# Sending token numbers instead of rows to the experts, moving the closing gate steps, and splitting HGRN's heads earlier

## The chip, the cores and the metric

The kernel runs on one core of a Trainium2 chip. The metric is the device time of one execution in microseconds (us); lower is better. The engines that appear below are PE (TensorE, the matrix multiplies), DVE (VectorE), ACT (ScalarE), POOL (GpSimd, which here mostly issues DMAs) and SP (SyncE, which issues DMAs). All five run their own instruction streams and wait for one another by semaphores.

## The reference, cut to what matters

A decoder trunk of two layers on 512 tokens of width 1024, in float32. Layer 0 is an mLSTM mixer and a dense SwiGLU; layer 1, where the change lies, is an HGRN2 mixer and a top-2-of-8 mixture of experts:

```python
# layer 1
o = hgrn2_chunkwise(q, k, log_f, v)                 # 8 heads of 128
o = head_rmsnorm(o, norm_w) * silu(g)
x = x + gate1 * (o @ w_out)                         # "h_out" below
t = rmsnorm(x, norm2_w) * (1 + scale2) + shift2
logits = t @ router_w                               # 512 x 8
top_logits, top_idx = top_k(logits, 2)
top_w = softmax(top_logits)
gates = sum_k top_w * one_hot(top_idx, 8)
y = sum_e gates[:, e] * ((silu(t @ wg[e]) * (t @ wu[e])) @ wd[e])
x = x + gate2 * y                                   # then the final norm
```

## The kernel before

**Precision and tiles.** Every float32 matmul is made of two halves: a tile is split into a high part (made by ACT: whi of a weight, hhi of a head) and a low part (made by DVE: wlo, hlo), and PE multiplies high x high, low x high and high x low. The residual stream x lies in DRAM and in SBUF as 8 tiles of 128 features x 512 tokens. Weights come from DRAM in tiles of two slots (1024 KB), are split slot by slot by ACT and DVE, and run ahead of PE by a fixed number of slots; SP issues these loads (L189, raw<-in_w or raw<-in_moe), in the order in which buffers come free. All engine instructions carry the line of a helper, L337; DMAs have lines of their own.

**HGRN.** `hgrn()` computes projections tile by tile (`proj`), and between them, a few instructions at a time, the recurrence of each head (`core`); `weave` sets that order by a cost estimate when the program is written out. The finished head `hh[h]` (normed, turned by tph, multiplied with g) is wanted by `h_out`, which takes the heads in order k = 0..7: first the product of each head with four of eight output tiles (12 matmuls of 128x512 per head), later with the other four. `heads()` hands them over: per head one ACT step (hhi), one DVE step (hlo), and one DMA on POOL that reloads the residual tile of that number (L1291, xr<-X).

**Route.** After h_out the residual is turned to token-major tiles xt (128 tokens x 512 features, 4 x 2 of them) and normed to zt by eight ACT steps (`pre_route`). `route` finds for each token its two experts and its rank within each; an expert has room for 152 rows (CAP), so there are 8 x 152 = 1216 slots (NSLOT), and each token has a row beyond them where a choice without a slot is dumped. `spread()` makes the row numbers `put` on DVE; then 16 indirect DMAs on POOL (4 token tiles x 2 halves x 2 choices) write 128 rows of 2 KB each of zt into XG, in DRAM (L1465), with a tiny memset (spacer, L1464) in front of each. XG was filled with zeros earlier, beside the projections (L1113, 20 DMAs). `rest()` makes what is wanted late: the gates of rows without a slot, their count (cps on PE, n_over), the gate matrix GM in DRAM (a DMA on POOL, L1497), and lists of rows for the final adding.

**Experts.** `experts` runs expert 0 to 7. Expert 0 gets its rows without DRAM, by a product of xt with one-hot matrices. A step (e, i) of the first part multiplies with the gate and up weights of the i-th tile of hidden features (gu, 16 pairs of matmuls for each of the two), i = 0..10; the second part multiplies down (yd). For expert e+1, `fetch` loads its 152 rows at (e, 4) from XG, as four direct DMAs of 76 x 512 (L1623, xr<-XG); the turns xT at (e, 7), (e, 8) and (e, 9) transpose them on PE, features 0 to 383, 384 to 767 and the others. The results go to Y in DRAM and at the end are gathered per token by 16 indirect DMAs of 128 rows (L1757, yg<-Y,relse).

Of the kernel before, what the change touches and what calls it, by code (L numbers as in the profile page):

```python
# [10 lines left out]
F32 = mybir.dt.float32  # L11
F32R = mybir.dt.float32r
BF16 = mybir.dt.bfloat16
I32 = mybir.dt.int32
U32 = mybir.dt.uint32
AF = mybir.ActivationFunctionType
OP = mybir.AluOpType
# [4 lines left out]
P = 128  # L22
D = 1024
T = 512
KT = D // P
NC = T // P
H = 8
# [4 lines left out]
NE = 8  # L32
# [48 lines left out]
PLAN, AT = _plan()  # L81
# [12 lines left out]

CAP = 152
NSLOT = NE * CAP
NROW = NSLOT + 2 * T
NY = NSLOT - CAP


# [307 lines left out]
class Kernel:  # L408
# [637 lines left out]
    def hgrn(self):  # L1046
        nc, tc = self.nc, self.tc
        V, S = nc.vector, nc.scalar
        ident = self.C("ident")
        with ExitStack() as ctx:  # L1050
# [9 lines left out]
            e = one.tile([P, 3, 8], F32, name="lbs")  # L1060
# [42 lines left out]
            def proj():  # L1103
                accs = self.group_first("h_first", 4, self.norm(1, 0))
                self.dump("hn1", [x for h in self.hn for x in h])
                for k in range(KT):
                    nc.gpsimd.dma_start(self.X[k], self.x[k])
                z = self.nrm.tile([P, T], F32, name="zero", tag="tmp")
                nc.gpsimd.memset(z, 0.0)
                for j in range(2):  # L1110
                    for i in range(0, NSLOT, P):
                        n = min(P, NSLOT - i)
                        nc.gpsimd.dma_start(self.XG[j][i:i + n], z[:n])  # L1113
                evac(0, (accs[:2], accs[2:]))
                self.router()
                yield
                for what in H_ORDER:
                    w, n = what[0], int(what[1])
                    ps = []
                    for i in range(4):  # L1120
                        acc = self.ps(f"h{what}{i}")
                        if w == "h":
                            yield from self.tile_ws(AT[what] + 8 * i, self.hn, acc)
                            ps.append(acc)
                            if i == 3:
                                while not done >= {n - 3, n - 4}:
                                    yield "wait"
                                evac(n, (ps[:2], ps[2:]))
                            continue
                        t = new(f"{what}{i}", "vg", 12)  # L1130
                        if w == "v":
                            yield from self.tile_tok(AT["h_" + what], i, acc)
                            S.activation(t, acc, AF.Copy)
                            v[n, i] = t
                        else:
                            yield from self.tile_ws(AT["h_" + what] + 8 * i, self.hn, acc)
                            S.activation(t, acc, AF.Copy)
                            g[n + i] = t
                            if i >= 2:
                                gated(range(n + (i - 2) * 3, n + i + 1))  # L1140
# [138 lines left out]
                else:  # L1279
                    S.activation(t, tp, AF.Copy, scale=self.V("hnw", h))  # L1280

            def heads():
                for h in range(H):
                    while h not in hh or h not in on:
                        yield None
                    hi = self.act.tile([P, T], F32R, name=f"hhi{h}", tag="act")
                    lo = self.act.tile([P, T], F32R, name=f"hlo{h}", tag="act")
                    S.activation(hi, hh[h], AF.Copy)
                    V.tensor_sub(lo, hh[h], hi.bitcast(F32))
                    self.x[h] = self.xp.tile([P, T], F32, name=f"xr{h}", tag="x")  # L1290
                    nc.gpsimd.dma_start(self.x[h], self.X[h])  # L1291
                    yield hi, lo

            out = self.out_proj("h_out", heads(), 1, lambda: next(self.side, None))

# [22 lines left out]
    def pre_route(self, pool, lps, xt):  # L1318

        nc = self.nc  # L1320
        ident = self.C("ident")
        tp = {}

        lgt = self.ps("lgt")

        rw4 = self.nrm.tile([P, T], F32, name="rw4", tag="rs", bufs=1)[:, :(KT - 1) * 32].rearrange("p (k c) -> p k c", c=32)
        nc.gpsimd.memset(rw4, 0.0)
        nc.gpsimd.tensor_copy(rw4[:, :, 0:NE], self.rwa[:, 0:KT - 1])
        fold = pool.tile([P, NE], F32, name="fold")
        nc.vector.tensor_reduce(fold, ident.rearrange("p (g j) -> p j g", g=4)[:, 0:NE], axis=AX.X, op=OP.add)  # L1330

        def logits(*ks):

            mm = nc.tensor.matmul
            if ks[0] < KT - 1:
                for k in ks:
                    mm(lgt[32 * (k % 4):32 * (k % 4) + 32], rw4[:, k], self.x[k], start=k < 4, stop=k + 4 >= KT - 1)
                return
            k = ks[0]
            for i in range(NC):  # L1340
                ts = slice(i * P, (i + 1) * P)
                mm(lps[:, i], self.lgs[:, ts], fold, start=i == 0, stop=False)
            for i in range(NC):
                ts = slice(i * P, (i + 1) * P)
                mm(lps[:, i], self.x[k][:, ts], self.rwa[:, k], start=False, stop=i == NC - 1)
            next(scale, None)

        def turn(k, i):
            if (i, k // 4) not in tp:
                tp[i, k // 4] = self.ps(f"xt{i}{k // 4}")  # L1350
            nc.tensor.transpose(tp[i, k // 4][:, (k % 4) * P:(k % 4 + 1) * P], self.x[k][:, i * P:(i + 1) * P], ident)

        def evac(i, j):
            xt[i][j] = self.act.tile([P, 512], F32, name=f"xt{i}{j}", tag="act")
            if i % 2 or j:
                nc.scalar.activation(xt[i][j], tp.pop((i, j)), AF.Copy)
            else:
                nc.vector.tensor_copy(xt[i][j], tp.pop((i, j)))

        for i in range(NC):  # L1360
            for k in range(4):
                turn(k, i)
            if i == NC - 1:
                logits(*range(4))
            yield
            evac(i, 0)
            yield
        scale = self.token_scale()
        for k in range(4, KT):
            if k == KT - 2:  # L1370
                logits(*range(4, KT - 1))
            elif k == KT - 1:
                logits(k)
            for i in range(NC):
                turn(k, i)
            if k == KT - 2:
                self.lgs = pool.tile([P, T], F32, name="lgs")
                nc.vector.tensor_copy(self.lgs, lgt)
                next(scale)
            if k < KT - 1:  # L1380
                yield
                yield
                yield
        zt = [[None, None] for _ in range(NC)]
        for i in range(NC):
            evac(i, 1)
        for i in range(NC):
            for j in range(2):
                zt[i][j] = self.act.tile([P, 512], F32, name=f"zt{i}{j}", tag="act")
                nc.scalar.activation(zt[i][j], xt[i][j], AF.Copy, scale=self.rs[:, i:i + 1])  # L1390
        self.zt = zt

    def route(self, pool, lps, xt):
# [48 lines left out]
        def spread():  # L1442
# [14 lines left out]
            V.tensor_tensor(d2, dump, ok, op=OP.mult)  # L1457
            V.tensor_sub(d2, dump, d2)
            V.tensor_add(put, sl, d2)
            last, spacer = [], t("spacer", shape=[1, 1])  # L1460
            for i in range(NC):
                for j in range(2):
                    for c in range(2):
                        nc.gpsimd.memset(spacer, 0.0)  # L1464
                        st = nc.gpsimd.indirect_dma_start(  # L1465
                            out=self.XG[j], out_offset=bass.IndirectOffsetOnAxis(ap=put[:, c, i:i + 1], axis=0),
                            in_=self.zt[i][j], in_offset=None)
                        for x in last:
                            tc.declare_no_dep(st.ins, x.ins, reason="other rows")
                        last.append(st)  # L1470
            gate = t("gate", shape=[P, 2, NC])
            ex, den = t("ex", shape=[P, NC]), t("den", shape=[P, NC])
            V.tensor_sub(ex, m2, m1)
# [135 lines left out]
    def experts(self, xp, hp, wk, xt, pick, rest):  # L1609
# [6 lines left out]
        def fetch(e):  # L1616

            rows[e] = [[self.xp.tile([P, T], F32, name=f"xr{q}{j}{e}", tag="x")[:HC] for j in range(2)]
                       for q in range(2)]
            for q in range(2):  # L1620
                r0 = e * CAP + q * HC
                for j in range(2):
                    nc.gpsimd.dma_start(rows[e][q][j], self.XG[j][r0:r0 + HC])  # L1623

        def place(e):
            xs[e] = xp.tile([P, KT, 2, CAP], F32R, name=f"x{e}", tag="x")
# [137 lines left out]
        for kind, e, i in moe_steps():  # L1764
            if kind == "g":
# [4 lines left out]
                        self.mm2(gu[u], W.get(b), xs[e][:, k], k == 0, k == KT - 1)  # L1770
                        b += 1
                act(e, i, gu)
                if (e, i) == (0, 1):
                    g, r, n_over = rest()
                if e + 1 < NE:
                    if i == 4:
# [84 lines left out]

    def run(self, stop=None):
        tc, nc = self.tc, self.nc
        self.XG = [self.dram.tile([NROW, 512], F32, name=f"XG{j}") for j in range(2)]
        self.Y = [self.dram.tile([NY, 512], F32, name=f"Y{j}") for j in range(2)]
        self.YL = self.dram.tile([CAP, 512], F32, name="YL")
        self.X = self.dram.tile([KT, P, T], F32, name="X")
# [76 lines left out]
```

## Time and profile before

| | us |
|---|---|
| median of 3 runs | 1553.86 |
| lowest and highest | 1550.51, 1555.45 |
| the profiled execution's own time | 1556.14 |
| its span in the trace | 1554.4 |
| PE busy | 1488.2 (96%) |
| DVE, ACT, POOL busy | 1087.0, 845.6, 133.5 |
| mean granted PE clock, share of full speed | 0.985 |

The span is what the trace shows, from the first instruction to the last; the profiled execution's own time is a little longer and is one run among others. Times in rows are microseconds from the start of the span. The HGRN mixer ends at about 900, the experts run from about 975 to 1530. DVE, ACT and POOL have idle time nearly everywhere, PE hardly any.

### The profile page before, as it was taken

Reading aid. Unit: us, or ns where it says so; the run is one execution under the profiler, and the core shown is the slowest. Engines: PE = TensorE matmul, PEld = TensorE weight load, DVE = VectorE, ACT = ScalarE, POOL = GpSimd, SP = SyncE. Lnnn points to the kernel's source line nnn. Section 1 sums busy time; section 2 is a strip of 40 time slices with the busy share of each in tenths; the row PEclk is TensorE's granted clock in tenths of the full one; section 3 lists DMA queues with packets and bytes.
Section 4 is the critical chain, followed back from the end, with each engine's and each line's share of the span. In section 5 each row is a group of like instructions: output and inputs, shape, how many; then the busy total and the mean of one; then the engine's idle time right before and its main releaser. Section 6 shows DMA issues by size and latency. Waiting matters only on the chain.

```text
span 1554.4 us, 23601 instructions
## 1 busy us (share of the span) xinstructions
PE 1488.2 (96%) x8955; PEld 1308.3 (84%) x8955; DVE 1087.0 (70%) x1992; ACT 845.6 (54%) x1561; POOL 133.5 (9%) x217
## 2 busy tenths in 40 slices
PE   4989999999999999999999999999999999999995
PEld 3867777888888888788888877899999999999984
DVE  6876774655455645695977755787887878788786
ACT  5466333432222322365656554687786868777663
POOL 0041000000000000310000020501000010100141
PEclk9999999999999999999999999999999999999997
DMA  9472551445445553542102152778787787878782
GB/s 373 168 207 80 202 176 64 167 176 216 161 164 205 180 197 109 201 146 101 55 28 82 55 207 94 251 246 294 267 277 275 275 279 252 294 266 269 278 305 92
DMA packets 80903, 300.47 MB, mean 193 GB/s; under 512 B 8085, under 2 KB 8133, under 8 KB 79761
## 3 DMA queue, kind: packets, MB, share of 16 engines
q1 hardware_dynamic: 68608, 263.21, 48.0%
q0 software_dynamic: 12176, 35.70, 6.9%
q8 instruction: 72, 1.18, 0.3%
q14 instruction: 47, 0.38, 0.1%
HBM read 280.78 MB, written 18.09 MB: 192 GB/s over the span
## 4 chain that ended last, share of the span: by engine, by line
PE 86%; DVE 6%; ACT 3%; DMA 3%; issue 1%; DVEq 0%; SPq 0%; ACTq 0%
PE gu L337 22%; PE yd L337 11%; PE fd L337 8%; PE fgp L337 7%; PE fup L337 7%; PE hh L337 4%; PE al L337 3%; PE hv L337 3%; PE h_out L337 3%; PE m_g L337 3%; PE m_out L337 2%; PE hg L337 2%; PE o L337 1%; DMA ar<-in_ada 1%; PE f_in L337 1%
## 5 line engine op out<-in xcount | busy, mean ns | idle before, releaser
L337 DVE TENSOR_TENSOR wlo<-raw,whi 128x1024 fp32r<-128x1024 f32 x403 | 489.5, 1222 | 104.0 <-ACT whi L337 99.4
L337 ACT ACTIVATE whi<-raw 128x1024 fp32r<-128x1024 f32 x403 | 421.9, 1054 | 171.2 <-DMA raw<-in_w 36.4
L337 PE MATMUL gu<-x,whi 128*128 128x304 f32 x1408 | 362.0, 346 | 2.8 <-issue 1.0
L337 PE MATMUL gu<-x,wlo 128*128 128x152 f32 x1408 | 330.6, 235 | 1.5 <-issue 1.4
L337 PEld LDWEIGHTS gu<-x,wlo 128*128 128x128 f32 x1408 | 271.4, 193 | 2.5 <-issue 2.3
L337 PEld LDWEIGHTS gu<-x,whi 128*128 128x128 f32 x1408 | 267.1, 190 | 3.4 <-issue 1.6
L337 PE MATMUL yd<-hb,whi 128*128 128x304 f32 x704 | 181.5, 347 | 1.9 <-DVE hb L337 1.9
L337 PE MATMUL yd<-hb,wlo 128*128 128x152 f32 x704 | 164.1, 233 | 0.0
L337 PEld LDWEIGHTS yd<-hb,wlo 128*128 128x128 f32 x704 | 134.7, 191 | 0.0
L337 PEld LDWEIGHTS yd<-hb,whi 128*128 128x128 f32 x704 | 132.4, 188 | 2.3 <-DVE hb L337 2.3
L337 DVE SCALAR_TENSOR_TENSOR ar<-ar,cond 128x1024 f32<-128x1024 f32 x80 | 97.3, 1219 | 3.0 <-DMA ar<-in_ada 2.9
L337 ACT ACTIVATE fhi<-fg 128x512 fp32r<-128x512 f32 x22 | 13.9, 633 | 114.3 <-DVE fg L337 114.3
L337 DVE TENSOR_TENSOR fg<-fg,fup 128x512 f32<-128x512 f32 x20 | 13.8, 688 | 82.7 <-PE fup L337 82.7
L337 ACT ACTIVATE t<-gu 128x152 f32<-128x152 f32 x176 | 48.3, 289 | 42.2 <-PE gu L337 35.8
L337 PE MATMUL fd<-fhi,whi 128*128 128x512 f32 x176 | 69.6, 396 | 0.0
L337 PE MATMUL fd<-flo,whi 128*128 128x512 f32 x176 | 69.6, 396 | 0.0
L337 PE MATMUL fd<-fhi,wlo 128*128 128x512 f32 x176 | 69.6, 396 | 0.0
L337 PE MATMUL fgp<-lo,whi 128*128 128x512 f32 x160 | 62.3, 389 | 0.0
L337 PE MATMUL fgp<-hi,whi 128*128 128x512 f32 x160 | 62.2, 389 | 0.0
L337 PE MATMUL fgp<-hi,wlo 128*128 128x512 f32 x160 | 62.2, 389 | 0.0
L337 PE MATMUL fup<-hi,whi 128*128 128x512 f32 x160 | 62.2, 389 | 0.0
L337 PE MATMUL fup<-lo,whi 128*128 128x512 f32 x160 | 62.2, 389 | 0.0
(413 smaller groups left out, 2978.0 us busy)
## 6 DMA issues: line engine op xcount, KB each, us to landing
raw<-in_moe SPq DMA_DIRECT2D x125, 1024.0 KB, 5.2
raw<-in_w SPq DMA_DIRECT2D x69, 1024.0 KB, 6.0
ar<-in_ada SPq DMA_DIRECT2D x80, 512.0 KB, 4.3
ad<-in_ada SPq DMA_DIRECT2D x8, 1024.0 KB, 15.3
XG<-zero POOLq DMA_DIRECT2D x18, 256.0 KB
xr<-XG POOLq DMA_DIRECT2D x28, 152.0 KB
raw<-in_moe SPq DMA_DIRECT2D x8, 512.0 KB, 3.6
Y<-yt POOLq DMA_DIRECT2D x14, 256.0 KB
```

The lines of the kernel that those rows point to most:

```text
L337: r = f(*args, **kw)
```

## The change

Five things change. (1) XG is gone. SP writes zt to ZT in DRAM by token (2 x 512 x 512), each 128 x 512 tile right after the ACT step that makes it. (2) A list L of 2304 int32 takes XG's place: it is zeroed by one small DMA; DVE makes the token numbers `tok`; eight indirect DMAs scatter 128 of these numbers each to the rows `put`; and one DMA on POOL loads the first 1216 back as `who` (76 x 16). (3) `fetch` gathers an expert's rows from ZT by `who`, four indirect DMAs of 76 rows. (4) `rest()` is called after step (1, 6) in place of (0, 1). (5) The split of a head moves to `halves`, called within the last g tile for heads 0 and 1, and then three heads ahead of the one that is handed over.

```diff
@@ proj
-                for j in range(2):
-                    for i in range(0, NSLOT, P):
-                        n = min(P, NSLOT - i)
-                        nc.gpsimd.dma_start(self.XG[j][i:i + n], z[:n])
+                nc.gpsimd.dma_start(self.L.rearrange("(p k) o -> p (k o)", p=P), z[:, :NROW // P].bitcast(I32))
...
-                            yield from self.tile_ws(AT["h_" + what] + 8 * i, self.hn, acc)
+                            for k, r in enumerate(self.tile_ws(AT["h_" + what] + 8 * i, self.hn, acc)):
+                                yield r
+                                if n and i == 3 and k > 1:
+                                    halves(k - 1)
@@ heads
-            def heads():
-                for h in range(H):
-                    while h not in hh or h not in on:
-                        yield None
+            parts = []
+            def halves(n):
+                for h in range(len(parts), min(n, H)):
+                    if h not in hh or h not in on:
+                        return
                     hi = self.act.tile([P, T], F32R, name=f"hhi{h}", tag="act")
                     lo = self.act.tile([P, T], F32R, name=f"hlo{h}", tag="act")
                     S.activation(hi, hh[h], AF.Copy)
                     V.tensor_sub(lo, hh[h], hi.bitcast(F32))
                     self.x[h] = self.xp.tile([P, T], F32, name=f"xr{h}", tag="x")
                     nc.gpsimd.dma_start(self.x[h], self.X[h])
-                    yield hi, lo
+                    parts.append((hi, lo))
+            def heads():
+                for h in range(H):
+                    while h not in hh or h not in on:
+                        yield None
+                    halves(h + 3)
+                    yield parts[h]
@@ pre_route
                 nc.scalar.activation(zt[i][j], xt[i][j], AF.Copy, scale=self.rs[:, i:i + 1])
+                nc.sync.dma_start(self.ZT[j][i * P:(i + 1) * P], zt[i][j])
@@ spread
+            tok = self.nrm.tile([P, NC], I32, name="tok", tag="ms", bufs=1)
+            V.tensor_scalar(tok, dump[:, 0], -float(NSLOT), None, op0=OP.add)
             for i in range(NC):
-                for j in range(2):
-                    for c in range(2):
...
-                            out=self.XG[j], out_offset=bass.IndirectOffsetOnAxis(ap=put[:, c, i:i + 1], axis=0),
-                            in_=self.zt[i][j], in_offset=None)
+                for c in range(2):
...
+                        out=self.L, out_offset=bass.IndirectOffsetOnAxis(ap=put[:, c, i:i + 1], axis=0),
+                        in_=tok[:, i:i + 1], in_offset=None)
...
+            self.who = t("who", I32, [CAP // 2, 2 * NE])
+            nc.gpsimd.dma_start(self.who, self.L[0:NSLOT].rearrange("(s p) o -> p (s o)", p=CAP // 2))
@@ fetch
-                    nc.gpsimd.dma_start(rows[e][q][j], self.XG[j][r0:r0 + HC])
+                    nc.gpsimd.indirect_dma_start(
+                        out=rows[e][q][j], out_offset=None, in_=self.ZT[j],
+                        in_offset=bass.IndirectOffsetOnAxis(ap=self.who[:, 2 * e + q:2 * e + q + 1], axis=0))
@@ the loop of experts
-                if (e, i) == (0, 1):
+                if (e, i) == (1, 6):
                     g, r, n_over = rest()
```

ACT's queue from the last g tile of HGRN on, before (g<-hg takes the projection out of PSUM, g<-g is its silu; the hhi are heads 0, 1 and 2 in turn):

```order
L337 ACTIVATE g_6875<-hg_6874 128x512
L337 ACTIVATE g_6875<-g_6875 128x512
L337 ACTIVATE hhi_6925<-hh_5253 128x512
L337 ACTIVATE whi_6934<-raw_6779 128x1024
L337 ACTIVATE qi,ssqh<-o_6837 128x128 x4
L337 ACTIVATE qi<-o_6837,rshy 128x128 x4
L337 ACTIVATE hhi_6968<-hh_5308 128x512
L337 ACTIVATE hhi_6991<-hh_5908 128x512
```

There the hhi of head 0 waits behind both steps on g. ACT's queue of the change at the same place:

```order
L337 ACTIVATE hhi_6893<-hh_5235 128x512
L337 ACTIVATE hhi_6907<-hh_5290 128x512
L337 ACTIVATE g_6857<-hg_6856 128x512
L337 ACTIVATE g_6857<-g_6857 128x512
L337 ACTIVATE hhi_6919<-hh_5890 128x512
L337 ACTIVATE whi_6928<-raw_6761 128x1024
L337 ACTIVATE qi,ssqh<-o_6819 128x128 x4
L337 ACTIVATE hhi_6949<-hh_6019 128x512
L337 ACTIVATE qi<-o_6819,rshy 128x128 x4
```

The hhi of heads 0 and 1 now stand ahead of the last g<-hg, and that of head 2 stands right behind g<-g; a split of a weight, the square sums of the last head (qi,ssqh) and its scaling (qi<-o,rshy) come after these.

PE's queue where the last head is turned (tph), before, at the end of h_out's first two heads:

```order
L337 MATMUL h_out_6924<-hhi_6968,whi_6703 128x512
L337 MATMUL h_out_6924<-hlo_6969,whi_6703 128x512
L337 MATMUL h_out_6924<-hhi_6968,wlo_6704 128x512
L337 MATMUL tph_6986<-cst_c,qi 128x128 x4
L337 MATMUL h_out_6921<-hhi_6991,whi_6781 128x512
L337 MATMUL h_out_6921<-hlo_6992,whi_6781 128x512
```

There the turn stands between the second and the third head. PE's queue of the change around the turn:

```order
L337 MATMUL h_out_6918<-hhi_6919,whi_6763 128x512
L337 MATMUL h_out_6918<-hlo_6920,whi_6763 128x512
L337 MATMUL h_out_6918<-hhi_6919,wlo_6764 128x512
L337 MATMUL tph_7002<-cst_c,qi 128x128 x4
L337 MATMUL h_out_6915<-hhi_6949,whi_6763 128x512
L337 MATMUL h_out_6915<-hlo_6950,whi_6763 128x512
```

The turn now follows the third head of h_out in place of the second.

POOL's queue around the first expert's fetch, before:

```order
L1465 DMA XG_79<-zt_7424,put 2240x512
L1464 MEMSET spacer 1x1
L1465 DMA XG_79<-zt_7424,put 2240x512
L1497 DMA GM<-gt 128x8x4
L1623 DMA xr_7877<-XG_78 76x512
L1623 DMA xr_7878<-XG_79 76x512
L1623 DMA xr_7879<-XG_78 76x512
```

There the four loads stand behind the last of 16 scatters and GM. POOL's queue of the change:

```order
L1479 DMA L<-tok,put 2304x1
L1478 MEMSET spacer 1x1
L1479 DMA L<-tok,put 2304x1
L1486 DMA who<-L 76x16x1
L1638 DMA xr_7818<-ZT_78,who 76x512
L1638 DMA xr_7819<-ZT_79,who 76x512
L1638 DMA xr_7820<-ZT_78,who 76x512
```

Eight scatters to the list are left; the load of `who` and the four gathers for expert 1 follow them, and GM<-gt is no longer between.

## Rows read from the trace of the kernel before

**Rows 1.** The page: busy time by engine; the chain that ended last.
```profile
PE 1488.2 (96%) x8955; PEld 1308.3 (84%) x8955; DVE 1087.0 (70%) x1992; ACT 845.6 (54%) x1561; POOL 133.5 (9%) x217
...
PE 86%; DVE 6%; ACT 3%; DMA 3%; issue 1%; DVEq 0%; SPq 0%; ACTq 0%
```

**Rows 2.** Windows: length; busy PE, PEld, DVE, ACT, POOL; granted clock; DMA share; GB/s.
```profile
655.00:660.00 5.00, 5.00 (x23) 4.03 (x22) 4.21 (x5) 1.76 (x3) 5.00 (x10) 1.00 0.96 348
900.00:910.00 10.00, 7.56 (x26) 5.04 (x25) 5.57 (x13) 7.83 (x21) 1.08 (x2) 0.83 0.45 143
965.00:970.00 5.00, 5.00 (x39) 5.00 (x40) 3.57 (x21) 2.26 (x7) 0.75 (x1) 1.00 0.00 0
980.00:985.00 5.00, 5.00 (x42) 4.86 (x41) 3.77 (x26) 3.99 (x6) 4.11 (x9) 1.00 0.50 194
985.00:1000.00 15.00, 12.88 (x74) 12.22 (x74) 11.32 (x21) 7.54 (x16) 8.91 (x15) 0.77 0.80 268
```

**Rows 3.** Timeline of PE, h_out's start: start, duration, instruction, [idle before, releaser].
```profile
899.97 0.39 PE L337 MATMUL o<-St,qi 128*128 128x128 f32 x2
901.77 0.50 PE L337 MATMUL h_out<-hhi,whi 128*128 128x512 f32 x1 [1.42 <-ACT hhi L337]
...
910.50 0.60 PE L337 MATMUL tph<-cst_c,qi 128*128 128x128 f32 x4
910.85 0.48 PE L337 MATMUL h_out<-hhi,whi 128*128 128x512 f32 x1
...
913.68 0.39 PE L337 MATMUL h_out<-hhi,whi 128*128 128x512 f32 x1
```

**Rows 4.** Timeline of ACT at the same place.
```profile
899.94 0.60 ACT L337 ACTIVATE g<-hg 128x512 f32<-128x512 f32 x1 [1.68 <-PE hg L337]
...
901.11 0.61 ACT L337 ACTIVATE hhi<-hh 128x512 fp32r<-128x512 f32 x1
...
905.38 1.14 ACT L337 ACTIVATE qi<-o,rshy 128x128 f32<-128x128 f32 x4 [1.69 <-DVE rshy L337]
```

**Rows 5.** Timeline of PE in expert 0.
```profile
988.54 0.34 PE L337 MATMUL gu<-x,whi 128*128 128x304 f32 x1
...
993.50 0.28 PE L337 MATMUL gu<-x,wlo 128*128 128x152 f32 x1 [0.51 <-issue]
993.58 0.55 PE L337 MATMUL gu<-x,whi 128*128 128x304 f32 x1
...
999.52 0.34 PE L337 MATMUL gu<-x,whi 128*128 128x304 f32 x1
...
999.77 0.34 PE L337 MATMUL gu<-x,whi 128*128 128x304 f32 x1
```

**Rows 6.** The tile zt: count, nanoseconds min/median/max, first and last start.
```profile
L1465 POOL DMA_INDIRECT XG<-zt,put x16: 966/1056/1964, 969.2 to 991.6; - x16
```

**Rows 7.** The tile yg, and the timeline of PE in expert 7 beside it.
```profile
L1757 POOL DMA_INDIRECT yg<-Y,relse x16: 944/1007/1917, 1472.7 to 1504.7; - x16
...
1488.50 0.34 PE L337 MATMUL gu<-x,whi 128*128 128x304 f32 x1
...
1489.65 0.39 PE L337 MATMUL gu<-x,whi 128*128 128x304 f32 x1 [0.49 <-issue]
...
1493.19 0.34 PE L337 MATMUL gu<-x,whi 128*128 128x304 f32 x1
```

**Rows 8.** Expert 2's fetch (POOL), a turn (PE), all early turns, and weight loads beside.
```profile
1068.25 2.11 POOL L1623 DMA_DIRECT2D xr<-XG  x4
...
1080.82 0.56 PE L337 MATMUL xT<-cst_c,xr 76*128 76x76 f32 x6
...
L337 PE MATMUL xT<-cst_c,xr x32: 227/228/233, 1012.8 to 1089.8; 76*128 76x76 f32 x32
...
raw<-in_moe SPq DMA_DIRECT2D x3, 1024.0 KB, 8.0
```

**Rows 9.** Timeline of DVE, the first of the closing gate steps.
```profile
980.80 0.17 DVE L337 TENSOR_SCALAR over<-rank 128x32 f32<-128x32 f32 x1
```

More of the change, by code (lines that the diff above doesn't have):

```diff
@@ L96 @@
 NSLOT = NE * CAP
-NROW = NSLOT + 2 * T
+NROW = -(-(NSLOT + 2 * T) // P) * P
 NY = NSLOT - CAP
@@ L1460, in spread @@
             last, spacer = [], t("spacer", shape=[1, 1])
+            tok = self.nrm.tile([P, NC], I32, name="tok", tag="ms", bufs=1)
+            V.tensor_scalar(tok, dump[:, 0], -float(NSLOT), None, op0=OP.add)
             for i in range(NC):
-                for j in range(2):
-                    for c in range(2):
-                        nc.gpsimd.memset(spacer, 0.0)
-                        st = nc.gpsimd.indirect_dma_start(
-                            out=self.XG[j], out_offset=bass.IndirectOffsetOnAxis(ap=put[:, c, i:i + 1], axis=0),
-                            in_=self.zt[i][j], in_offset=None)
-                        for x in last:
-                            tc.declare_no_dep(st.ins, x.ins, reason="other rows")
-                        last.append(st)
+                for c in range(2):
+                    nc.gpsimd.memset(spacer, 0.0)
+                    st = nc.gpsimd.indirect_dma_start(
+                        out=self.L, out_offset=bass.IndirectOffsetOnAxis(ap=put[:, c, i:i + 1], axis=0),
+                        in_=tok[:, i:i + 1], in_offset=None)
+                    for x in last:
+                        tc.declare_no_dep(st.ins, x.ins, reason="other rows")
+                    last.append(st)
+            self.who = t("who", I32, [CAP // 2, 2 * NE])
+            nc.gpsimd.dma_start(self.who, self.L[0:NSLOT].rearrange("(s p) o -> p (s o)", p=CAP // 2))
             gate = t("gate", shape=[P, 2, NC])
@@ L1620, in fetch @@
             for q in range(2):
-                r0 = e * CAP + q * HC
                 for j in range(2):
-                    nc.gpsimd.dma_start(rows[e][q][j], self.XG[j][r0:r0 + HC])
+                    nc.gpsimd.indirect_dma_start(
+                        out=rows[e][q][j], out_offset=None, in_=self.ZT[j],
+                        in_offset=bass.IndirectOffsetOnAxis(ap=self.who[:, 2 * e + q:2 * e + q + 1], axis=0))
         def place(e):
@@ L1863, in run @@
         tc, nc = self.tc, self.nc
-        self.XG = [self.dram.tile([NROW, 512], F32, name=f"XG{j}") for j in range(2)]
+        self.ZT = [self.dram.tile([T, 512], F32, name=f"ZT{j}") for j in range(2)]
+        self.L = self.dram.tile([NROW, 1], I32, name="L")
         self.Y = [self.dram.tile([NY, 512], F32, name=f"Y{j}") for j in range(2)]
```

## The prediction

> **What bounds the kernel now.** I read the page's first and fourth parts first: TensorE (PE) is busy 96% of the span and holds 86% of the chain that ended last [rows 1]. What is moved or removed beside a full PE is worth nothing; a change is worth what it takes out of PE's own idle or slow stretches. So I next read busy time and granted clock in stretches from the HGRN mixer on [rows 2]. At 655, 965 and 980 PE is busy for 5.00 of 5.00 us at clock 1.00. In two stretches it is not, and the change touches both: 900 to 910, where h_out starts (7.56 of 10.00 at 0.83), and 985 to 1000, in expert 0 (12.88 of 15.00 at 0.77). The timelines of PE and ScalarE (ACT) there [rows 3 to 5] give what can be won. The rest of the diff is searched for what it can lose.
>
> **1. Heads split ahead.** PE's last work of the mixer starts at 899.97 and takes 0.39 us, so it ends at 900.36; h_out's first matmul waits 1.42 us for ACT's hhi, to 901.77 [rows 3]. That hhi starts only at 901.11, behind the two steps on the last g tile, though its head had been finished long before; ACT sat idle 1.68 us ahead of those two [rows 4]. The second head's hhi stands behind ACT's wait of 1.69 us for rshy and the four qi steps from 905.38 on. So 24 matmuls and the turn tph last from 900.36 to 910.85. The third head then takes 12 matmuls without a wait, 910.85 to 913.68, which is 0.236 us each [rows 3]. After the change PE has 36 matmuls ahead of tph: 900.45 + 36 x 0.236 = 908.95, and with the turn's 0.35 us (910.85 - 910.50) the fourth head starts at 909.3 in place of 913.68. The gain is **4.4 us**, of which the clock's fall in this stretch is a part: without the pause I expect no fall.
>
> What is late next: the third head's hhi, now third on ACT, starts at about 901.1 and is wanted at 900.45 + 24 x 0.236 = 906.1. tph wants the four qi steps, which ended at 905.38 + 1.14 = 906.5 before and have one hhi (0.61) and one hlo more ahead of them, so 907.8 at worst, against 908.95. Neither is late. If the two hhi ahead of g<-hg take ACT's 1.2 us out of the path instead of out of its idle time, 3.2 us are left; that and 4.4 are the ends, and I take 4.4, since the idle 1.68 us stand in the row. From here on PE is full and the gain stays. The reloads of X go with the split, two of them now ahead of POOL's constants and weight fetch; at some 0.53 us of issue each (a quarter of the 2.11 in [rows 8]) that is 1.1 us on a queue that reads for expert 0, more than 50 us later. 0.
>
> **2. Four bytes scattered in place of rows.** GpSimd (POOL) sends off 16 scatters of 128 rows of 2 KB between 969.2 and 992.6 [rows 6], beside the stream of weights. Towards their end PE stands still with no semaphore behind it ("issue", the last of them 0.51 us in front of 993.50), and then runs slow [rows 5]. A pair of matmuls (whi, wlo) takes 999.77 - 999.52 = 0.25 us at full speed. From 988.54 to 993.58 seven pairs take 5.04 us, 3.3 too many; from 993.58 to 999.52 thirteen take 5.94, 2.7 too many, the granted clock being down after the standstill (0.77 over the stretch [rows 2]). Together 6.0 us. The only other place in the experts where PE has such idle time is at 1489.65, and it lies in the only other long series of indirect row transfers, 16 gathers from 1472.7 to 1504.7 [rows 7]; by the same count 10 pairs take 4.7 us there, 2.2 too many. At 655 the DMA share is 0.96 by direct transfers and PE doesn't stall [rows 2]. I take it that a long series of indirect row transfers makes the stall, and that eight scatters of 512 bytes in all, over some ten microseconds sooner, don't: **6.0 us** gained; 0 if I have the cause wrong.
>
> The Trainium skill (Runtime: NRT & Kernel Launch, "Instruction fetch mechanics") says that instructions reach an engine in blocks of 16 KiB by a DMA queue of its own, and that this is mostly hidden. If that holds here, the standstill isn't a late block of instructions, the tie to the row transfers is weaker, and the sum would be that of rival A; no wait in the trace names that queue.
>
> The rows go to DRAM by token instead, eight DMAs of 256 KB from SP's queue right behind the zt steps. The DMA share is 0.00 at 965 [rows 2]: 0. One small DVE step for the token numbers (0.17, as the first in [rows 9]) lies ahead of ex on the way to the gates, which scale the experts' output and not expert 0's input: 0, at most 0.2. The fill with zeros loses 20 DMAs, at 655, where PE was full: 0.
>
> **3. Gathers by the list.** For expert 1 the way is longer: scatters from 964.8 (969.2 less 4.4) for about 8 x 1.3 = 10.4 us, to 975.2; some 3 us to land; `who`, 1216 separate numbers, some 8 us as the longest landing in [rows 8]; four gathers at 1.3, to 991.4, landed by about 999. The first turn, now at 1012.8 [rows 8], comes 10.4 us sooner, at 1002.4. It holds, with 3 us in hand. For experts 2 to 7 `who` is there, and four indirect gathers, a median 1.01 us and at most 1.92 each [rows 7], with 0.3 between two, take the place of 2.11 us for four direct loads [rows 8]. The first turn needs the third: issued by 1068.25 + 3 x 1.01 + 0.6 = 1071.9, 8.9 us ahead of the turn at 1080.82. A load of 1024 KB lands in a median of 8.0 [rows 8]; 152 KB in less. So 0. The other end: each issue takes 1.92 and lands after 8.0, that is 1068.25 + 6.4 + 8.0 = 1082.6, 1.8 late, 12.6 us over seven experts. I take 0, as the median is the nearer row.
>
> The Trainium skill (DMA: Bandwidth & Descriptors, "Rules for kernel authors") says that a transfer whose last dimension isn't contiguous goes down as one descriptor per element, and asks to rearrange it. The load of `who` is of that form and nothing in this trace is; by that rule it would be slower than a row load of its size, and eat from expert 1's margin.
>
> **4. Closing gate steps.** 22 DVE steps from 980.80 [rows 9], some 4.2 us, go from expert 0 to expert 1. In expert 0 PE was busy 5.00 of 5.00 beside them, at 980 [rows 2]: their going gives 0, and as expert 1's weights are split at the same pace, their coming costs 0. From above it is 4.2, if nothing of the splitting runs ahead there. The sum over the overflow (cps) on PE follows them and is asked for a whole group of matmuls later: 0.
>
> **Sum**, against the profiled execution's 1556.14 us (its span is 1554.4, it lies 2.28 above the median 1553.86): 1556.14 - 4.4 - 6.0 = 1545.7, and from the median 1543.5. I say **1544.5**, between the two.
>
> **Rivals.** A. *The stall in expert 0 stays*, because it comes of the weight stream together with any series of indirect transfers, and `who` and four gathers still follow the eight scatters: -4.4 alone, 1549.5 to 1551.7. For it speaks that the cause is read from two places only; against it, that the rows, 4 MB, are gone from that time. B. *The early split gives nothing*, PE finding another wait at h_out's start: -6.0 alone, 1547.9 to 1550.1. Against it: ACT's idle time stands in its row. C. *Gathers come somewhat late*, by half of the bound above: 1543.5 + 6.3 = 1549.8, up to 1556. D. *Slower: the stall comes with every expert's gathers.* The mechanism of part 2 seven times over, at 2.2 us as at 1489.65: 15.4 - 10.4 = 5.0 more, 1558.9 to 1561.1, and at 6.0 each 1585. It decides from (10.4 + 4.7) / 7 = 2.2 us per expert on. For it: row gathers are just what now runs beside a full weight stream. Against it: in both long series PE ran on through the first ten or more transfers, and here four come at a time.
>
> **How the numbers follow.** Forecast 0.62, A 0.14, B 0.09, C 0.09, D 0.06. A measurement tells about 0.3% here, 4.7 us: faster is below 1549.2, slower above 1558.5. Faster: the 0.62, 0.07 of B, 0.03 of A and 0.03 of C, 0.75 in all. Slower: D and 0.01 of C, 0.07. Same: 0.18. The range goes down to 1541, the 1543.5 with most of the spread that the runs show (1550.51 to 1553.86), and up to 1551.5, the upper end of A and B; D and the most of C lie outside, and little on the lower side.
>
> **What would show it.** Right: h_out's matmuls follow the last o without idle time, and the stretch from 900 on reads full at clock 1.00; the stretch at 980 to 1000 has PE full at 1.00; no idle time of PE in front of xT in experts 1 to 7. Wrong: "issue" in expert 0 still (A); a wait or the low clock at h_out still (B); PE waiting in front of xT for a gather (C); "issue" behind each expert's gathers (D); PE waiting for split weights in expert 1 (part 4).

## The result, and the profile after

| | us |
|---|---|
| before, median of 11 runs | 1553.42 |
| after, median of 11 runs | 1561.84 (1556.87 to 1574.91) |
| ratio after to before, 95% interval | 1.0057 (1.0041 to 1.0073) |
| profiled execution of after: time, span | 1561.84, 1560.1 |

The change makes the kernel 0.6% slower, about 8 us; faster was forecast, 1544.5 us, with 1551.5 as the upper end. Both gains of the prediction are in the trace. They are given back by waits for the gathered rows. The page of after, busy time and chain, against [rows 1]:

```profile
PE 1489.2 (95%) x8955; PEld 1310.3 (84%) x8955; DVE 1089.5 (70%) x1993; ACT 845.0 (54%) x1561; POOL 145.0 (9%) x183
...
PE 66%; issue 17%; DVE 6%; DMA 4%; ACT 3%; POOL 2%; DVEq 0%; SPq 0%; POOLq 0%; ACTq 0%
```

PE does the same work in a longer span; in the chain PE's share has fallen from 86% to 66%, "issue" has risen from 1% to 17%, and POOL has come in. The windows of after (columns as in [rows 2]) say where:

```profile
655.00:660.00 5.00, 5.00 (x23) 3.98 (x22) 4.13 (x5) 1.67 (x2) 0.54 (x1) 1.00 0.19 58
900.00:910.00 10.00, 10.00 (x47) 8.27 (x46) 6.49 (x16) 7.92 (x21) 2.62 (x5) 1.00 0.66 215
965.00:970.00 5.00, 4.55 (x36) 4.37 (x34) 1.30 (x3) 3.23 (x9) 4.12 (x9) 1.00 0.02 0
980.00:985.00 5.00, 5.00 (x42) 5.00 (x42) 4.61 (x9) 4.74 (x11) 0.00 (x0) 1.00 1.04 227
985.00:1000.00 15.00, 15.00 (x122) 15.00 (x122) 13.23 (x25) 10.99 (x22) 5.50 (x4) 1.00 0.99 285
1000.00:1010.00 10.00, 8.00 (x57) 7.85 (x57) 5.68 (x11) 5.64 (x15) 0.00 (x0) 0.83 0.77 263
1140.00:1150.00 10.00, 7.96 (x53) 7.80 (x53) 5.72 (x10) 6.07 (x13) 0.00 (x0) 0.83 0.81 250
1350.00:1360.00 10.00, 7.34 (x49) 7.18 (x49) 5.13 (x9) 5.87 (x13) 0.00 (x0) 0.83 0.87 271
```

The stretches from 900 and from 985, which had 7.56 of 10.00 and 12.88 of 15.00 before, are full at clock 1.00. (965 has less PE only because the same work stands 5 us earlier there; the turns for expert 0 have the same waits for DVE as before.) The three new ones are where PE begins to turn the rows of experts 1, 3 and 6. The waits of PE in the experts, summed by releaser, of before and of after:

```profile
PE gu L337 <- issue: 2.4, 6, 0.7
PE yd L337 <- DVE hb L337: 1.9, 2, 1.3
```

```profile
PE xT L337 <- DMA xr<-ZT,who: 8.8, 5, 2.7
PE yd L337 <- DVE hb L337: 1.8, 2, 1.3
PE gu L337 <- issue: 0.8, 3, 0.5
```

Of the 2.4 us of "issue" before, 1.7 lay in expert 0 and 0.7 in expert 7; the 0.8 that are left lie in expert 7 (1492 to 1498). The five waits for gathered rows in PE's timeline of after (start, duration, instruction, idle time before it):

```profile
1003.29 0.55 PE L337 MATMUL xT<-cst_c,xr 76*128 76x76 f32 x5 [2.00 <-DMA xr<-ZT,who]
...
1144.09 0.55 PE L337 MATMUL xT<-cst_c,xr 76*128 76x76 f32 x5 [2.04 <-DMA xr<-ZT,who]
...
1214.88 0.28 PE L337 MATMUL xT<-cst_c,xr 76*128 76x76 f32 x1 [0.93 <-DMA xr<-ZT,who]
...
1284.43 0.55 PE L337 MATMUL xT<-cst_c,xr 76*128 76x76 f32 x5 [1.21 <-DMA xr<-ZT,who]
...
1355.44 0.55 PE L337 MATMUL xT<-cst_c,xr 76*128 76x76 f32 x5 [2.66 <-DMA xr<-ZT,who]
```

The waits sum to 8.8 us. Behind the three of 2 us and more the granted clock goes to half for about 3.4 us (0.83 over each 10 us); behind the two shorter ones it doesn't. In the slow stretch a pair of matmuls takes 0.467 us in place of 0.25, as between these two starts of a whi:

```profile
1007.11 0.54 PE L337 MATMUL gu<-x,whi 128*128 128x304 f32 x1
1007.58 0.54 PE L337 MATMUL gu<-x,whi 128*128 128x304 f32 x1
```

That is 1.6 us each, 4.7 in all. So 13.5 us are read off directly. By the starts of the gu steps, after stands 11.7 us ahead of before at step (0, 7), 997.06 against 1008.78, and 4.0 behind at (6, 0), 1370.10 against 1366.12: 15.7 us. The closing gate steps have 0.7 of it (below). The steps with a wait, and the next ones where the clock fell, have 14.7: each wait costs some 0.2 us more than itself. In expert 7's last part another 1.5 us go to one more fall of the clock, at 1514; the profiles of other runs differ there by as much.

### The profile page after: what moved, and what is told of

The parts are those of the page before. It is cut to its first block, busy times and chain, and to the rows that moved or that the text cites. A ratio compares the mean times of both kernels' runs of the same rounds, so it can differ in the third digit from the quotient of the medians.

```text
span 1560.1 us, 23581 instructions
## 1 busy us (share of the span) xinstructions
PE 1489.2 (95%) x8955; PEld 1310.3 (84%) x8955; DVE 1089.5 (70%) x1993; ACT 845.0 (54%) x1561; POOL 145.0 (9%) x183
## 4 chain that ended last, share of the span: by engine, by line
PE 66%; issue 17%; DVE 6%; DMA 4%; ACT 3%; POOL 2%; DVEq 0%; SPq 0%; POOLq 0%; ACTq 0%
PE gu L337 9%; PE fd L337 8%; PE fgp L337 7%; PE fup L337 7%; PE yd L337 6%; PE hh L337 4%; PE al L337 3%; PE hv L337 3%; PE h_out L337 3%; PE m_g L337 3%; PE m_out L337 2%; PE hg L337 2%; POOL xr L1638 2%; PE o L337 1%; DMA xr<-ZT,who 1%
```

## The experiments

Ratios are to the kernel before, run beside it on the same chip, with 95% intervals.

**1. The early split alone.** The kernel before with `halves` and nothing else:

```diff
...
                 for h in range(H):
                     while h not in hh or h not in on:
                         yield None
+                    halves(h + 3)
+                    yield parts[h]
...
```

> The kernel before with the early split of the heads alone. In the trace of the whole change everything behind h_out stood 4.8 us earlier than before, counted from the end of the HGRN mixer. If the split does this alone and PE stays full up to the end: 4.8 us less, a ratio of 0.997. If what is won is given back somewhere before the end: 1.000.

Measured: 1548.05 us, ratio 0.9959 (0.9942 to 0.9975). The interval holds the 4.9 us that the trace of the change shows for the split (below): it is not given back.

**2. List and gathers alone.** The change without the split and with `rest()` back behind (0, 1):

```diff
...
-                if (e, i) == (1, 6):
+                if (e, i) == (0, 1):
                     g, r, n_over = rest()
```

> The change without its early split and with the closing gate steps back in expert 0: token list, ZT and gathers alone. Theory (late gathers cost about 15 us, the standstill of expert 0 that goes gives 6): about 9 us more than before, a ratio of 1.006, with PE waiting for the gathers in front of xT in about five of seven experts and no standstill at slot 4 of expert 0. Rival (the waits in front of xT come of the 4.8 us by which the split moves things, or of the gate steps in expert 1): a ratio below 1.000.

Measured: 1572.44 us, ratio 1.0112 (1.0090 to 1.0135), slower still than the 1.006 expected. The waits in front of xT come with the gathers, and are worse here: 14.2 us in six experts.

```profile
PE xT L337 <- DMA xr<-ZT,who: 14.2, 6, 4.2
```

So neither the 5 us of the split nor the gate steps make them.

**3. The fetch earlier.** The whole change with one line moved:

```diff
-                    if i == 4:
+                    if i == (2 if e else 4):
                         fetch(e + 1)
```

> The whole change, with the fetch for experts 2 to 7 called after step (e, 2) in place of (e, 4), some 34 us sooner; that for expert 1 stays. Theory (the gathers are only late, and nothing else is wrong with them): the waits in front of xT of experts 2 to 7 go, with the low clock behind them; 1561.8 less about 11 to 13, 1549 to 1551; expert 1's wait of 2 us stays. Rival (the gathers take from PE whatever their time, by stalls or by holding up the weights): no better than 1559.

Measured: 1548.13 us, ratio 0.9944 (0.9921 to 0.9966). Only expert 1's wait, 1.8 us, is left, and no fall of the clock follows it: the gathers do PE no harm but by coming late. In this kernel the tile xr tells how they go, at their earlier place; the columns are nanoseconds min/median/max of an issue on POOL, and below, us from issue to landing:

```profile
L1638 POOL DMA_INDIRECT xr<-ZT,who x28: 1122/1738/1914, 990.5 to 1339.2; - x28
...
DMA to landing us min/median/max: 6.8/9.8/12.6
```

**4. Direct loads at the same place.** The whole change, but

```diff
-                    nc.gpsimd.indirect_dma_start(
-                        out=rows[e][q][j], out_offset=None, in_=self.ZT[j],
-                        in_offset=bass.IndirectOffsetOnAxis(ap=self.who[:, 2 * e + q:2 * e + q + 1], axis=0))
+                    nc.gpsimd.dma_start(rows[e][q][j], self.ZT[j][(2 * e + q) * 24:(2 * e + q) * 24 + HC])
```

> The whole change, but each fetch loads 76 neighbouring rows of ZT by four direct DMAs, with no list in it, so that the experts work on rows that aren't theirs; everything else stays, the list too. Theory (it is the indirect form that is late, by its slower issue on POOL and its slower landing beside the weights): no wait in front of xT in any expert, 1545 to 1548, and direct loads that land some 6 us after issue where the gathers take 10. Rival (any load at this place is late, since the whole comes 5 to 12 us earlier against a stream of weights that doesn't): waits of 1 to 2 us stay, 1555 or more.

Measured: 1546.09 us, ratio 0.9935 (0.9915 to 0.9954), and no wait in front of xT. The same tile (26 of the 28 loads):

```profile
L1638 POOL DMA_DIRECT2D xr<-ZT x26: 525/536/577, 984.6 to 1403.5; - x26
...
DMA to landing us min/median/max: 3.4/7.4/12.7
```

The indirect form is dearer to issue, 1.7 us against 0.54, and lands later, 9.8 us against 7.4. The second is the weaker reading. Other gathers of 76 rows landed in medians of 9.0 us (experiment 2, of the landings that its trace tells) and 8.3 (experiment 8, second kernel), and when this kernel was run again (experiment 7) the direct loads took 8.3, still without a wait.

**5. Why late: the count of rows.** Two kernels change only how many rows a gather takes, 128 in the first, as shown, and 80 in the second (the rows beyond 76 aren't used):

```diff
-            self.who = t("who", I32, [CAP // 2, 2 * NE])
+            self.who = t("who", I32, [128, 2 * NE])
...
-                        name=f"xr{q}{j}{e}", tag="x")[:HC]
+                        name=f"xr{q}{j}{e}", tag="x")[:128]
...
```

> The whole change, but each gather takes 128 rows in place of 76 (the list is loaded with overlap; the 52 rows behind an expert's own aren't used). The gathers of 76 rows take 1.13 to 1.91 us to issue (median 1.89), those of 128 rows at the end of the kernel a median of 1.01. Theory (the dear issue comes of a count of rows that isn't a multiple of 16 or doesn't fill the partitions): issue falls to about 1.0 us, the third gather goes off 2.6 us sooner, and most waits in front of xT shrink, unless the 1.7 times as many bytes take it back; 1553 to 1558. Rival (the issue waits for the queue that the weights fill, whatever the count): issue stays near 1.9, waits grow, 1562 or more.

> The whole change with gathers of 80 rows in place of 76 (the 4 rows behind an expert's own part aren't used). If a multiple of 16 rows is what makes the issue cheap: about 1.0 us per gather, and shorter waits in front of xT. If it is the whole of 128 partitions, or the queue: near 1.9 as with 76.

Measured: with 128 rows 1546.18 us, ratio 0.9940 (0.9915 to 0.9966); with 80 rows one execution of 1542.26. With 128 rows PE waits for no gather, although they bring 1.7 times the bytes; but the theory named the wrong half. The issue stays dear (medians 1.71 and 1.66 us; Part 3 below says what it stands behind); it is the landing that is shorter, at 128 and, in the second fence, at 80 rows:

```profile
L1639 POOL DMA_INDIRECT xr<-ZT,who x28: 953/1713/1917, 991.2 to 1409.0; - x28
...
DMA to landing us min/median/max: 4.2/7.0/8.0
```

```profile
L1639 POOL DMA_INDIRECT xr<-ZT,who x28: 909/1659/1911, 983.6 to 1403.6; - x28
...
DMA to landing us min/median/max: 4.3/7.6/9.3
```

The packets tell the two kinds apart. From 1128 to 1144, around expert 3's fetch, the DMA view of the change (76 rows) and of the kernel with 80:

```profile
DMA packets 1776, 4.56 MB, mean 285 GB/s; under 512 B 660, under 2 KB 660, under 8 KB 1775
...
q0 software_dynamic: 848, 0.94, 24.5%
```

```profile
DMA packets 1471, 5.12 MB, mean 320 GB/s; under 512 B 193, under 2 KB 193, under 8 KB 1470
...
q0 software_dynamic: 400, 0.97, 21.0%
```

The four gathers of 76 rows come with some 450 more packets in POOL's queue, all tiny, and with 76 direct rows there are none either (202 packets under 512 B in the same window of experiment 4). The packets and the lateness went together with these rows; that the packets make the lateness is not shown by itself.

For expert 1 something else changed too. The list is loaded to 128 or 80 partitions here, and that load takes 1.24 and 0.99 us to issue, where 76 partitions took 2.2. With 80 rows the first gather starts some 17 us ahead of expert 1's first turn, in the change 12.9. So expert 1's wait went partly by the list; those of experts 3 to 6 can't have.

**6. 80 rows, timed, and with the early fetch.**

> The gathers of 80 rows once more, timed (one execution gave 1542.3). Theory (76 rows land late because they go off with some 430 extra packets of 8 bytes a fetch, and 80 rows without): a ratio of 0.992 to 0.995, and no wait over 0.5 us in front of xT. Rival (that one execution was a lucky one, and the count of rows isn't the cause): 1.000 or more, with waits of 1 to 2 us again.

> Gathers of 80 rows and the early fetch for experts 2 to 7 together. Theory: with 80 rows nothing is left for the early fetch to win, the same time as the run before on that chip, within 1.5 us. Rival (80 rows still come late in part of the executions): 2 to 4 us less than without the early fetch.

Measured: 1546.18 us, ratio 0.9953 (0.9934 to 0.9971), and 1545.62, ratio 0.9946 (0.9928 to 0.9964). One wait of 0.35 us is left in front of xT in the first, none in the second. Four more rows per gather take the loss away; an earlier fetch then wins nothing that can be told from noise.

**7. The standstill of expert 0.** The kernel before, profiled again:

> The kernel before, unchanged, profiled a second time. Theory of the prediction (the long series of row scatters makes the standstill in expert 0): PE stands still again at slot 4 of expert 0, some 3 us, with the low clock behind it, 6 us in all. Rival (the standstill is an accident of one execution, since the kernel with the early split alone has the same scatters and none): no standstill there, a span near 1549.

It stands still again (1559.59 us), in the same step of expert 0 and with the same mark; PE's timeline:

```profile
994.07 0.23 PE L337 MATMUL gu<-x,wlo 128*128 128x152 f32 x1 [0.84 <-issue]
995.47 0.30 PE L337 MATMUL gu<-x,whi 128*128 128x304 f32 x1 [1.18 <-issue]
996.20 0.23 PE L337 MATMUL gu<-x,wlo 128*128 128x152 f32 x1 [0.42 <-issue]
```

Then experiment 4's kernel with the row scatters put back in place of the eight small ones:

```diff
             for i in range(NC):
-                for c in range(2):
-                        out=self.L, ... in_=tok[:, i:i + 1]
+                for j in range(2):
+                    for c in range(2):
+                        out=self.XG[j], ... in_=self.zt[i][j]
```

> The whole change with direct loads in the fetch, as in the run before on that, and in place of the eight scatters of numbers the 16 scatters of 2 KB rows of the kernel before, at the same place in POOL's queue; the list stays zero and the experts work on rows that aren't theirs. Theory (row scatters beside the weight stream cost 6 us on PE): a ratio of about 0.9935 + 0.004 = 0.997 to 0.998, and a standstill without a semaphore in expert 0. Rival (they cost nothing by themselves): 0.9935, and no standstill.

Measured: 1550.30 us, ratio 0.9943 (0.9922 to 0.9964), with the standstill in its profile (2.2 us of "issue", five places). Against experiment 4's 1546.09 us and 0.9935, taken at another time, that decides nothing, so the pair was run once more, side by side on one chip:

> The run with direct loads in the fetch once more (whole change, no list in the fetch, the experts work on rows that aren't theirs), on one chip with the next one, in more rounds. Beside that: theory (row scatters cost PE some 6 us) this one is 4 to 7 us below the next; rival (what the profiles show isn't in most executions) at most 2 us below.

> The run with 16 scatters of 2 KB rows in place of eight of numbers once more (direct loads in the fetch, the list stays zero, the experts work on rows that aren't theirs). Theory: 4 to 7 us above the one before it here, and the standstill in expert 0 in its profile; rival: at most 2 us above.

Measured: 1546.45 us (0.9940, 0.9918 to 0.9963) without and 1550.99 (0.9974, 0.9956 to 0.9992) with row scatters: 4.5 us, within the 4 to 7 of the theory, though the two intervals still overlap a little. This time the profile with row scatters has no standstill; PE pays in another place, for expert 1's direct loads, which queue behind the scatters:

```profile
1006.27 0.55 PE L337 MATMUL xT<-cst_c,xr 76*128 76x76 f32 x5 [2.73 <-DMA xr<-ZT]
```

Experiment 1 has row scatters too and only 0.77 us of that. So of five profiles with row scatters three have the standstill, and of the eleven without row scatters, the change's own among them, none at that place. By the lengths of expert 0's steps the five lost 6.0, 7.7, 1.0, 5.9 and 5.0 us (before, again, experiment 1, and the two of this experiment). Rival A is out. A block of instructions that comes late isn't seen either: the DMA view lists no packet of an instruction queue from 980 to 997 in the kernel before, from 985.5 to 1004 when it was profiled again and from 982 to 994 in this experiment's first kernel, and PE stands still inside these stretches.

**8. A list in two parts.** With the early fetch, the numbers of expert 1 are loaded first, the others behind its gathers, once with the gate steps back in expert 0 and once where the change has them:

```diff
-            nc.gpsimd.dma_start(self.who, self.L[0:NSLOT].rearrange(...))
+            nc.gpsimd.dma_start(self.who[:, 2:4], self.L[CAP:2 * CAP].rearrange(...))
...
+            if e == 1:
+                nc.gpsimd.dma_start(self.who[:, 4:], self.L[2 * CAP:NSLOT].rearrange(...))
```

> The whole change with the early fetch for experts 2 to 7, the gate steps back behind step (0, 1), and the list loaded in two parts: the 152 numbers of expert 1 first, the others behind expert 1's gathers. Theory (expert 1 waits 1.9 us for its rows because the load of all 1216 numbers takes 7 to 8 us to land): the smaller load lands some 4 us sooner, the wait in front of expert 1's first turn goes, and with the gate steps 0.5 us: 2 to 4 us less than with the early fetch alone, a ratio of 0.992. Rival (the small load lands no sooner, being held by the weights in the queues): no difference.

> The whole change with the early fetch for experts 2 to 7 and the list loaded in two parts, the gate steps in expert 1 as the change has them. In the run with those steps back in expert 0, PE waited 0.82 us for their count there, and gave back what the steps had cost in expert 1. Theory: no wait in front of expert 1's first turn, none for the count, 0.8 us in expert 1; a ratio of 0.992 to 0.993, below both kernels and about with the direct loads. Rival (expert 1's wait comes back, its list being late again): 0.9945.

Measured: 1547.01 us, 0.9940 (0.9917 to 0.9962), and 1546.55, 0.9952 (0.9934 to 0.9970). Expert 1's wait is gone in both; in the first of them the first gather goes off at 982.33, in the change at 988.15. In time neither can be told from the early fetch alone; the 0.992 expected of both was not reached. In the first, PE waited 0.82 us for the count of the gate steps instead. In the second's profile the clock falls in expert 7 (0.66 from 1500 to 1510), as in those of experiments 1 and 5 (128 rows) and others, and not in those of experiments 2 to 4; its span says little of expert 1.

## Why the prediction was wrong

**Part 1, heads ahead: right.** Predicted 4.4 us. In after h_out starts right behind the mixer, where [rows 3] has a wait for ACT:

```profile
899.34 0.39 PE L337 MATMUL o<-St,qi 128*128 128x128 f32 x2
899.49 0.48 PE L337 MATMUL h_out<-hhi,whi 128*128 128x512 f32 x1
...
908.12 0.48 PE L337 MATMUL h_out<-hhi,whi 128*128 128x512 f32 x1
```

The mixer ends at 899.73, 0.63 sooner, which is less than the 2 us by which the two profiles of the kernel before differ there, and the fourth head starts at 908.12 in place of 913.68: 5.56 less 0.63 is 4.9 us. ACT's two hhi lie in its idle time, as assumed. Experiment 1 measured 0.9959, 6.4 us with an interval of 3.9 to 9.0: nothing of it was given back, so rival B is out.

**Part 2, the standstill: right in kind, and near in size.** Predicted 6.0 us, and the profile of after has steps (0, 3) and (0, 4) 6.0 us shorter than before; in timed executions row scatters cost 4.5 us (experiment 7). So the exact 6.0 is in part luck of the two profiles. That a series of row transfers stops PE's issue is one of two forms that the cost takes, not the rule. What exactly holds up PE there stays open; nothing that the trace names releases it.

**Part 3, gathers: the step that failed.** The prediction took 0, "as the median is the nearer row", and kept 12.6 us as the other end; 13.5 to 15 came. Both durations in that step were borrowed from rows of another shape. The issue was put at 1.01 us, the median of gathers of 128 rows at the end of the kernel [rows 7]; it measured 1.89 in after, almost the 1.92 that had been kept as the worst. The rows of after show what an issue stands behind: 22 of the 28 gathers start while DVE is in a wlo step (the split of a weight), and these end 0.99 to 1.08 us after that step does; the six others take 1.13 to 1.29 us. The third gather for expert 3, with DVE's step:

```profile
1133.10 1.23 DVE L337 TENSOR_TENSOR wlo<-raw,whi 128x1024 fp32r<-128x1024 f32 x1 [0.35 <-ACT whi L337]
...
1133.85 1.48 POOL L1638 DMA_INDIRECT xr<-ZT,who  x1 [0.30 <-issue]
```

The step ends at 1134.33, the gather's issue at 1135.33. The gathers at the kernel's end did the same already before: seven of the 16 started in a wlo step and ended 0.82 to 1.05 us after it, the others took 0.94 to 1.04. The direct loads took 0.53 to 0.60 us whatever DVE did. No run moves DVE's work to test this. The landing was put under the 8.0 us of a 1024 KB load [rows 8], since 152 KB is less. In after it can be read from the third gather, which the first turn needs; for expert 3 it starts at 1133.85 and for expert 6 at

```profile
1344.56 1.49 POOL L1638 DMA_INDIRECT xr<-ZT,who  x1 [0.30 <-issue]
```

and PE gets its rows 10.2 and 10.9 us later, for experts 4 and 5 after 9.1 and 9.4; 8.2 would have been in time. (Why experts 2 and 7 had no wait, and 1, 3 and 6 the longest, stays open.) Size was the wrong scale: what counted was the number of rows, 76 in place of 80 or 128, with the many more packets that go with it. With the dear issue alone (80 rows, experiments 5 and 6) PE waited at most 0.35 us, so the margin had room for the issue, not for both. A cheap issue with the slow landing wasn't tried; by an estimate from these rows, two gathers issued at 1.01 us in place of 1.9 send the third off 1.8 us sooner, and 0.2 and 0.9 us of wait would be left for experts 3 and 6. The tile xr of after, and its list:

```profile
L1638 POOL DMA_INDIRECT xr<-ZT,who x28: 1130/1886/1910, 988.2 to 1417.9; - x28
L1486 POOL DMA_DIRECT2D who<-L x1: 2215/2215/2215, 977.6 to 977.6; - x1
```

For expert 1, where 3 us were said to be in hand, `who` was issued at 977.58, about when the prediction had it (978), but the first gather followed only at 988.15, 10.6 us later in place of 8; the rows came 2.0 us late.

The Trainium skill (DMA: Bandwidth & Descriptors, "Rules for kernel authors") says that a transfer whose last dimension isn't contiguous goes down as one descriptor per element; the prediction set that against the load of `who`. The profiles don't show descriptors. They agree that this load is slow for its 4.8 KB: it lands 9.4 to 12.2 us after its issue (experiments 3, 4 and 7), about as late as the 152 KB loads that follow it. Its issue doesn't go by the count of numbers: 2.2 us for 1216 of them to 76 partitions (1.1 for 152 of them), 0.99 for 1280 to 80, 1.24 for 2048 to 128. It was a small part of the loss, since it touches expert 1 alone.

**Part 4, the closing gate steps: nearly right.** Predicted 0. A gu step is 16 pairs of matmuls, eight for gate and eight for up, 4.00 us at 0.25. In after steps (1, 6) and (1, 7) last 4.21 and 4.54 us in place of 4.00 and 4.36, and (2, 0) 4.32 in place of 4.00, while (0, 1) and (0, 2) have 4.00 each in place of 4.21 and 4.07: 0.7 lost, 0.3 won.

**The rivals and the range.** What happened is rival C, but at more than twice its price, and so with the sign of D; D's own mechanism, a standstill without a semaphore behind each expert's gathers, shows in no profile. C was priced at half of its bound and given 0.09, and the range, which ended at 1551.5, left most of it out although its own bound, 1543.5 + 12.6, reached 1556. The fall of the clock behind a wait, which was written into part 1 and part 2, was left out of part 3. With the bound taken whole C would have read 1556, and with the 4.7 us of the three falls that came, 1561.

## What to carry to other kernels

A transfer that takes the place of another in front of a deadline needs a row of its own form: an indirect gather of 76 rows is neither a direct load of its size nor a gather of 128. Where there is none, put the request earlier by the whole unknown: here an earlier place in the program was enough (0.9944 in place of 1.0057). And count behind a wait on a busy PE the slow stretch that can follow: in the change the waits of 2.0 to 2.7 us cost 3.8 to 4.5, those of 0.9 and 1.2 only 0.2 more than themselves.

## What the runs showed of the hardware

Gathers of 76 rows carry some 110 packets of under 512 B each that gathers of 80 and 128 rows don't. They landed beside the weights in medians of 8.3 to 9.8 us, against 7.3 to 7.6 with 80 rows and 7.0 with 128; 80 and 128 are multiples of 16 and 76 is not, though other counts weren't tried. Direct loads of 76 rows have no such packets and took 6.7 to 8.4 us, so the two forms overlap in landing. The issue of a gather on POOL took a median of 1.7 to 1.9 us in the experts and 1.0 in the series at the kernel's end; nearly all the difference is that the gathers in the experts mostly start inside a wlo step of DVE and end some 1.0 us (76 rows), 0.79 (80) or 0.85 (128) after it. A direct load took 0.54 at any time. The load of the list took 2.2 us to issue to 76 partitions, and 1.0 and 1.2 us to 80 and 128, with more numbers.
